# Latent-attention heads turned in groups of 128 columns in a two-layer encoder trunk

## The chip, the cores and the metric

The kernel runs on one core of a Trainium2 chip. The metric is the device time of one execution in microseconds (us), the median of several runs. A profiled execution gives the trace from which the rows are quoted. Its span is the time from the first to the last recorded instruction; the time of the execution is a little longer than its span.

The engines are called as the profile calls them: PE (TensorE, matrix products), PEld (its weight loads, which overlap the products), ACT (ScalarE), DVE (VectorE), POOL (GpSimd), SP (SyncE, which issues the loads). PE writes to PSUM, which has eight banks of 128 partitions x 512 floats; ACT and DVE copy results from there to SBUF, POOL works in SBUF alone.

## The reference

One sequence of 512 tokens with 1024 features goes through two layers. All of it is float32.

```python
h = rms_norm(x, attn_norm_g[l])
proj = h @ w_in[l]
c_q, c_kv, k_rope, gq, gk, gv, pool_in, gate_logits = split_columns(proj, IN_SIZES)
o_mla  = mla_branch(...)     # latent attention, 8 heads
o_gqa  = gqa_branch(...)     # 8 query heads of 64, 2 key heads
o_pool = pool_branch(...)    # centred means over 2/4/8/16 tokens, minus the token
gates = sigmoid(gate_logits).reshape(b, s, 3, d)
merged = sum of gates[:, :, i] * (branch i @ its projection)
x = x + merged @ w_out[l]
hf = rms_norm(x, ffn_norm_g[l])
u = depthwise_conv(hf @ ffn_w_up[l], ffn_conv_w[l], ffn_conv_b[l])
x = x + (silu(u_gate) * u_val) @ ffn_w_down[l]
```

In the latent attention each head of q and of k has 96 features, 64 without position and 32 rotary ones:

```python
q = (rms_norm(c_q, q_norm_g) @ w_uq).reshape(b, s, 8, 96)
kv = (rms_norm(c_kv, kv_norm_g) @ w_ukv).reshape(b, s, 8, 64 + 64)
k_nope, v = kv[..., :64], kv[..., 64:]
k = concatenate([k_nope, k_rope for every head], axis=-1)
q = rms_norm(q, qh_g); k = rms_norm(k, kh_g)
q, k: the last 32 features rotated by the token's row and column
o = softmax(q k^T * 96 ** -0.5) v
```

## The kernel before

Every product is made from halves: an operand is rounded to a shorter format (the high half, by a copy on ACT or DVE, line 208 or 231), and the rest is subtracted (the low half, on DVE or POOL, line 215 or 219). `mm3` then issues three matmuls: high x high, high x low, low x high. Weights are loaded as `raw` by SP, split into `wh` and `wl` by `w_split` some pieces ahead, and used once. Activations lie as feature x token in XM, HH (high) and HL (low), in eight chunks of 128 features.

A layer goes through these stages. First the latents: eight chunks of weights times HH and HL into four banks, token x feature. Then four groups of the pool branch; in layer 0 the sum of squares for the first norm (`norm_finish`, a product of `ones` with `sq`) is put between the matmuls of the first group, because the norm's factor is applied to results only afterwards. `rt` is that factor per token, `rbc` the same spread over partitions. Then the latents are normed (`mx`) and turned, and the grouped-query columns follow. Then comes grouped-query attention, beside which PE works on the gates and projection of the pool branch; then latent attention, beside which it works on those of the grouped-query branch; then the last gates, the output projection, the convolution network.

For latent attention `make_q` and `make_n` write the heads, token x feature, to MQ and MK, two tiles of four heads each, in time with the gates before. `q_norm` and `k_norm` scale them and apply the rotation on POOL. `t_q(h)` and `t_k(h)` later turn one head into features x tokens: four transposes of 128 tokens each into the one bank `mi`, then a high half (`qa`, `kh`) and a low half (`qb`, `kl`). `gcol` is a factor per feature put on q when it is copied. `m_row` uses the same bank for the row of the scores' maxima. `t_pair` does the same for two heads of the grouped-query branch, whose 128 columns are turned at once.

The order of the instructions is written out by the program itself: a model of the engines' times (`Clock`) keeps a heap of due steps; `chain` runs a list of steps one after the other, `need` waits until a result is due, `ps(tag)` until a bank of that tag is free. The list `plan` in `attention` gives a position for each step of each head. Between steps, units of the gates and branches (`Filler`) are issued up to a target, and up to SLACK = 35 units beyond it while the next step's inputs are not yet due. `copy` puts a copy on ACT or on DVE, whichever the model has free earlier, and `pick` does so with a low half between DVE and POOL. Banks: two each of `acc`, `ST` and `AV`, one each of `S` and `mi`. Each engine runs its own instructions strictly in the order in which the program issued them.

Of the kernel before, what the change touches and what calls it, by code (L numbers as in the profile page):

```python
# [18 lines left out]
P = 128  # L19
# [37 lines left out]
def _order(br):  # L57
# [189 lines left out]
def trunk(ctx: ExitStack, tc: tile.TileContext, x, w, prm, gb, cst, out):  # L247
# [41 lines left out]
    def f(ap):  # L289
        return ap.bitcast(F32)  # L290
# [14 lines left out]
    def w_split():  # L305
        j = st["split"]
        sl, off, wd = pieces[j]
        r = raws[sl][:, off:off + wd]
        hi = hlp.tile([P, T], F32R, tag="wh", name=f"wh{j}")
        lo = hlp.tile([P, T], F32R, tag="wl", name=f"wl{j}")  # L310
        ck.fin = ck.now
        A.activation(hi[:, :wd], r, AF.Copy)
        e = V if j < KC + 3 else pick(W_BIAS, ck.fin + ck.SEM)
        ck.free[e.kind] = max(ck.free.get(e.kind, 0.0), ck.fin + ck.SEM)
        e.tensor_tensor(lo[:, :wd], r, f(hi[:, :wd]), ALU.subtract)
        done("w", j)
        halves[j] = (hi, lo)
        st["split"] += 1
# [191 lines left out]
    def layer(l, sq, xsrc):  # L510
# [9 lines left out]
        tabs = [slot("tabg"), slot("tabg")]  # L520
        tabm = slot("tabm")

        gcol = small("gcol", [P, 1], bufs=1)

        def tables():
            V.tensor_tensor(gcol[0:96], pr[0:96, PRM_MQ:PRM_MQ + 1], pr[0:96, PRM_MQ + 1:PRM_MQ + 2], ALU.mult)
            V.tensor_scalar(gcol[0:64], gcol[0:64], 96.0 ** -0.5, None, ALU.mult)
            V.tensor_scalar(gt[:, 0:128], gt[:, 0:128], 64.0 ** -0.5, None, ALU.mult)
# [398 lines left out]

        def q_norm(g):
            q = MQ[g]
            qr = q[:, :, :, 64:96]  # L930
            cs, sn = (tabm[:, o:o + 128].rearrange("p (b f) -> p b f", b=4)[:, :, None, :] for o in (0, 128))
            r2 = slot("rp2")[:, :T].rearrange("p (b h f) -> p b h f", b=4, h=4)
# [5 lines left out]
            def part(o, i):  # L938
                G.tensor_tensor(r2[:, :, :, o:o + 16], qr[:, :, :, i:i + 16], bc(sn[:, :, :, o:o + 16], [P, 4, 4, 16]),
                                ALU.mult)  # L940

            return [lambda: scale(0), lambda: scale(1), lambda: part(0, 16), lambda: part(16, 0),
                    lambda: G.tensor_tensor(qr, qr, bc(cs, [P, 4, 4, 32]), ALU.mult),
                    lambda: G.tensor_tensor(qr, qr, r2, ALU.add), lambda: done("mq", l, g)]

        def make_n(g):
            wh, wl = wnext()
# [24 lines left out]
        def n_out(g, p, acc):  # L972
            j = slot("mns")
            bs = slice(2 * p, 2 * p + 2)

            def copies():
                copy(MK[g][:, bs, :, 0:64], acc.rearrange("p (b h f) -> p b h f", b=2, h=4))
                A.activation(j[:, :T], acc, AF.Square)
                free("acc")

            def sums():
                V.tensor_reduce(ss[:, 1, g, bs], j[:, :T].rearrange("p (b h f) -> p b h f", b=2, h=4), AX.X, ALU.add)
                done("ssn", l, g, p)

            chain(copies, sums)

        def k_norm(g):
            k = MK[g]

            def nope(p):  # L990
                bs = slice(2 * p, 2 * p + 2)
                G.tensor_tensor(k[:, bs, :, 0:64], k[:, bs, :, 0:64], bc(ss[:, 1, g, bs].unsqueeze(3), [P, 2, 4, 64]),
                                ALU.mult)

            def rope():
                G.tensor_tensor(k[:, :, :, 64:96], bc(krr[:, :, None, :], [P, 4, 4, 32]),
                                bc(ss[:, 1, g].unsqueeze(3), [P, 4, 4, 32]), ALU.mult)

            return [([("krr", l)], rope), lambda: nope(0), lambda: nope(1), lambda: done("mk", l, g)]

# [36 lines left out]
        def attention(kind, fill, okey, odst):  # L1037
# [7 lines left out]
            def t_q(h):  # L1045
                if gqa:
                    return t_pair(h) if h % 2 == 0 else None
                s = hs[h] = {}
                tp = ps("mi")
                need(("mq", l, h // 4))  # L1050
                for b in range(4):
                    turn(tp[0:96, b * P:b * P + P], MQ[h // 4][:, b, h % 4, :])
                qa, qb = s["qa"], s["qb"] = slot("qa", F32R), slot("qb", F32R)

                def hi():
                    A.activation(qa[0:96, :T], tp[0:96], AF.Copy, scale=gcol[0:96])

                def lo():
                    V.scalar_tensor_tensor(qb[0:96, :T], tp[0:96], gcol[0:96], f(qa[0:96, :T]), ALU.mult, ALU.subtract)
                    free("mi")  # L1060
                    done(*key("q", h))

                chain(hi, lo)

            def t_pair(h):

# [6 lines left out]
                for i in range(2):  # L1073
# [18 lines left out]
            def t_k(h):  # L1092
                if gqa:
                    return
                s = hs[h]
                need(("mk", l, h // 4))
                tp = ps("mi")
                for b in range(4):
                    turn(tp[0:96, b * P:b * P + P], MK[h // 4][:, b, h % 4, :])
                ka, kb = s["ka"], s["kb"] = slot("kh", F32R), slot("kl", F32R)  # L1100

                def hi():
                    copy(ka[0:96, :T], tp[0:96])
                    G.memset(f(ka[96:100, :T]), 1.0)
                    done(*key("kh", h))

                def lo():
                    V.tensor_tensor(kb[0:96, :T], tp[0:96], f(ka[0:96, :T]), ALU.subtract)
                    free("mi")
                    done(*key("kl", h))  # L1110

                chain(hi, lo)

            def s_max(h, b):
                s = hs[h]
# [365 lines left out]
def _pack_weights(i):  # L1481
    res = []
    for l in range(L):
# [16 lines left out]
        for br in (2, 1, 0):  # L1500
            for k, m in _order(br):
# [3 lines left out]
                elif k == "b":  # L1505
                    res += _cut(_blocks(wb[br][:, c], 4))
                elif k == "q":
                    res += [uq[kc * P:kc * P + P, m * 384:m * 384 + 384] for kc in range(2)]
# [19 lines left out]
def _pack_params(i):  # L1528
# [3 lines left out]
    def ones_after(v):  # L1532
# [3 lines left out]
    prm = np.concatenate([cols(i["attn_norm_g"]), cols(i["ffn_norm_g"]), cols(i["pool_scale"]),  # L1536
                          cols(i["mla_q_norm_g"]), cols(i["mla_kv_norm_g"]),
                          cols(cw[:, 0]), cols(cw[:, 1]), cols(cw[:, 2]), cols(i["ffn_conv_b"]),
                          cols(ones_after(i["mla_q_head_g"])), cols(ones_after(i["mla_k_head_g"]))], axis=2)

    def swap(v):
        n = v.shape[1] // 2
# [56 lines left out]
```

## Time and profile before

| | |
|---|---|
| median of 3 runs | 1649.69 us (1648.71 to 1650.75) |
| the profiled execution, its time | 1649.25 us |
| its span | 1647.3 us |
| granted TensorE clock | 1.00 |
| instructions | 20363 |
| PE matmuls | 7435 |
| POOL busy | 921.9 us (56%) |
| DMA queue of the weights | 143.97 MB, 27.6% of 16 engines |

The stages lie about here (us of the span): latents, pool and grouped-query columns 0 to 98, grouped-query attention to 212, latent attention 226 to 354, the rest of layer 0 up to 819; layer 1 repeats it. In a timeline row the columns are start, duration, engine, line, operation, output<-inputs, shape, count, and in brackets how long the engine was idle before and for whom. A matmul's duration overlaps that of the next; what a matmul costs is the distance between two starts. In a row of waits stand who waited and for whom, us in total, times, and the longest.

### The profile page before, as it was taken

What the parts mean: (1) busy time and instruction counts of PE and PEld (TensorE: products, weight loads), DVE (VectorE), ACT (ScalarE), POOL (GpSimd) and SP (SyncE); (2) the same over time, 40 slices, a digit from 0 to 9 for tenths busy, and PEclk for the clock granted to TensorE, in tenths of its full rate; (3) what the DMA queues carried; (4) which work ended last, traced back from release to release, by engine and by line L of the source; (5) the groups of instructions that cost most, each with busy time, mean ns of one, the idle gap of its engine ahead of it and who ended that gap; (6) DMA issues with size and microseconds to landing.
All of it is one profiled execution on the core that took longest, in us unless ns stands there. A gap on an engine that the chain in (4) does not pass through costs nothing.

```text
span 1647.3 us, 20363 instructions
## 1 busy us (share of the span) xinstructions
PE 1640.4 (100%) x7435; PEld 1336.7 (81%) x7435; DVE 890.5 (54%) x1404; ACT 761.8 (46%) x1357; POOL 921.9 (56%) x805
## 2 busy tenths in 40 slices
PE   9999999999999999999999999999999999999999
PEld 8887887778888888888888888877788888888888
DVE  6777756643366666621046677566332666666000
ACT  6457745543444444432244577455434444444221
POOL 3762763344666666654568538534446656656542
PEclk9999999999999999999999999999999999999999
DMA  5221121123322323333332211211243232332331
GB/s 201 82 84 46 60 65 48 52 71 118 119 90 90 103 90 91 102 102 122 102 103 89 82 39 62 74 39 52 85 133 95 85 103 90 91 101 90 126 111 45
DMA packets 44739, 145.40 MB, mean 88 GB/s; under 512 B 5088, under 2 KB 6624, under 8 KB 44640
## 3 DMA queue, kind: packets, MB, share of 16 engines
q1 hardware_dynamic: 44352, 143.97, 27.6%
q8 instruction: 59, 0.97, 0.2%
q14 instruction: 40, 0.33, 0.1%
q10 hardware_dynamic: 288, 0.14, 0.0%
HBM read 139.90 MB, written 4.19 MB: 87 GB/s over the span
## 4 chain that ended last, share of the span: by engine, by line
PE 98%; DVE 1%; ACT 1%; DMA 0%; SPq 0%; issue 0%
PE ps_acc L344 44%; PE ps_AV L344 24%; PE ps_ST L344 23%; PE ps_S L344 4%; PE ps_mi L344 2%; PE ps_mi L348 1%; DVE sq L215 0%; DMA XM<-x 0%; ACT wh L208 0%; ACT sqt L208 0%; DVE wl L215 0%; PE ps_acc L348 0%; SPq L301 0%; ACT HH L208 0%; SPq L1439 0%
## 5 line engine op out<-in xcount | busy, mean ns | idle before, releaser
L215 POOL TENSOR_TENSOR wl<-raw,wh 128x512 fp32r<-128x512 f32 (+2 forms) x508 | 662.9, 1315 | 589.0 <-ACT wh L208 457.7
L208 ACT ACTIVATE wh<-raw 128x512 fp32r<-128x512 f32 (+3 forms) x522 | 308.8, 607 | 125.6 <-PE ps_ST L344 41.1
L219 DVE SCALAR_TENSOR_TENSOR a<-u,prm,a 128x512 f32<-128x512 f32 x176 | 238.9, 1358 | 79.4 <-ACT a L208 73.2
L344 PE MATMUL ps_acc<-HH,wh 128*128 128x512 f32 x592 | 234.7, 396 | 1.4 <-DVE XM L219 1.4
L344 PE MATMUL ps_acc<-HL,wh 128*128 128x512 f32 x592 | 234.6, 396 | 0.0
L344 PE MATMUL ps_acc<-HH,wl 128*128 128x512 f32 x592 | 234.2, 396 | 0.0
L344 PEld LDWEIGHTS ps_acc<-HH,wh 128*128 128x128 f32 x592 | 111.5, 188 | 28.5 <-ACT mqs L208 1.7
L344 PEld LDWEIGHTS ps_acc<-HH,wl 128*128 128x128 f32 x592 | 111.3, 188 | 26.3
L344 PEld LDWEIGHTS ps_acc<-HL,wh 128*128 128x128 f32 x592 | 111.5, 188 | 25.5
L208 ACT ACTIVATE ps_ST<-ps_ST 128x512 f32<-128x512 f32 x128 | 74.6, 583 | 113.5 <-PE ps_ST L344 113.0
L344 PE MATMUL ps_AV<-HL,wh 128*128 128x512 f32 x288 | 114.2, 396 | 0.0
L344 PE MATMUL ps_AV<-HH,wl 128*128 128x512 f32 x288 | 114.2, 396 | 0.0
L344 PE MATMUL ps_AV<-HH,wh 128*128 128x512 f32 x288 | 113.6, 394 | 0.0
L223 DVE TENSOR_REDUCE nm<-ps_S 128x1 fp32r<-128x512 f32 x128 | 87.8, 686 | 42.4 <-PE ps_S L344 41.1
L215 DVE TENSOR_TENSOR pl<-ps_ST,ph 128x512 fp32r<-128x512 f32 x128 | 87.7, 685 | 38.4 <-ACT ph L208 37.4
L215 POOL TENSOR_TENSOR al<-a,ah 128x512 fp32r<-128x512 f32 x44 | 58.2, 1322 | 84.9 <-ACT ah L208 58.6
L344 PE MATMUL ps_ST<-HL,wh 128*128 128x512 f32 x240 | 95.3, 397 | 0.0
L344 PE MATMUL ps_ST<-HH,wl 128*128 128x512 f32 x240 | 95.0, 396 | 0.0
L344 PE MATMUL ps_ST<-HH,wh 128*128 128x512 f32 x240 | 94.6, 394 | 0.0
L208 ACT ACTIVATE a<-u,prm 128x512 f32<-128x512 f32 x88 | 71.8, 815 | 33.4 <-DVE u L215 33.4
L208 ACT ACTIVATE ah<-a 128x512 fp32r<-128x512 f32 x44 | 27.8, 631 | 116.0 <-DVE u L243 110.6
L208 ACT ACTIVATE a<-a 128x512 f32<-128x512 f32 x44 | 27.8, 632 | 113.0 <-DVE u L243 113.0
(361 smaller groups left out, 3543.8 us busy)
## 6 DMA issues: line engine op xcount, KB each, us to landing
raw<-w SPq DMA_DIRECT2D x228, 512.0 KB, 3.5
raw<-w SPq DMA_DIRECT2D x13, 384.0 KB, 3.1
XM<-x SPq DMA_DIRECT2D x16, 256.0 KB, 4.1
raw<-w SPq DMA_DIRECT2D x6, 448.0 KB, 3.4
xsp<-XM SPq DMA_DIRECT2D x8, 256.0 KB, 2.0
XM<-xsp SPq DMA_DIRECT2D x8, 256.0 KB, 3.4
out<-XM SPq DMA_DIRECT2D x7, 256.0 KB, 2.1
raw<-w SPq DMA_DIRECT2D x4, 432.0 KB, 3.1
```

The lines of the kernel that those rows point to most:

```text
L208: return self.eng.activation(out, in_, func, **k)
L215: return self.eng.tensor_tensor(out, *a)
L219: return self.eng.scalar_tensor_tensor(out, *a)
L223: return self.eng.tensor_reduce(out, in_, *a, **k)
L344: PE.matmul(o, lhsT=lhsT, rhs=rhs, start=start, stop=stop)
L348: PE.transpose(o, src, ident)
```

## The change

Six things are changed.

1. `t_q` and `t_k` turn the columns of four heads in three groups of 128 and not in four of 96. The head h with h % 4 == 3 has no transposes of its own. A group holds one whole head and a third of the next (group 0), two thirds of two heads (group 1), or a third of one and a whole head (group 2). TURNS lists for each group which head gets which rows, and at which row of the head they go. In every second head the 32 rotary columns stand ahead of the other 64, so that all pieces begin at a multiple of 32 and end up in the same rows of the head as before. The weights of q are permuted for that outside the kernel; for k, `parity` picks the columns.
2. All high halves of a group are made first, then all low ones, in one chain; then the bank is freed. The pieces of 32 rows of q have no factor, the others take it from `gcol`, which gets a second column in the groups' order.
3. `q_norm` and `k_norm` do on POOL in two steps, for even and odd heads, what was one step: for q both parts of the rotation, the product with the cosines and the sum, for k the scaling. The copies of k into MK are split in the same way.
4. The two copies per pair of grouped-query heads (`t_pair`) are always on ACT, not on ACT or DVE.
5. In layer 0 the norm's sum comes after six chunks of the first pool group, not four.
6. The high half of the very first piece of weights is made on DVE, not ACT, and the twelve products of the first chunk are issued as four high x high, four low x high, four high x low, and not bank by bank.

```diff
-NPRM = PRM_MQ + 2
+NPRM = PRM_MQ + 4
+TURNS = (((0, 0, 96, 0), (1, 96, 128, 64)), ((1, 0, 64, 0), (2, 64, 128, 0)),
+         ((2, 0, 32, 64), (3, 32, 64, 64), (3, 64, 128, 0)))
 # w_split
-        A.activation(hi[:, :wd], r, AF.Copy)
+        if j == 0:
+            V.tensor_copy(hi[:, :wd], r)
+        else:
+            A.activation(hi[:, :wd], r, AF.Copy)
 # tok_major
+                if st["use"] == 1:
+                    for n, (x_, w_) in enumerate(((HH, wh), (HL, wh), (HH, wl))):
+                        for b in range(4):
+                            mm(banks[b][:, :wd], x_[:, kc, b * P:b * P + P], w_[:, :wd], n == 0, False)
+                    continue
 # layer, the pool groups
-                if l == 0 and g == 0 and n == 3:
+                if l == 0 and g == 0 and n == 5:
                     norm_finish(G1, sq, nrm)
 # q_norm
+            def part(o, j):
...
+                for i in range(2):
+                    G.tensor_tensor(hold[0][:, i, :, :, o:o + 16], pair(i)[:, :, :, j:j + 16],
+                                    bc(sn[:, :, :, o:o + 16], [P, 4, 2, 16]), ALU.mult)
+            def turned():
+                for i in range(2):
+                    G.tensor_tensor(pair(i), pair(i), bc(cs, [P, 4, 2, 32]), ALU.mult)
+            def add():
+                for i in range(2):
+                    G.tensor_tensor(pair(i), pair(i), hold[0][:, i], ALU.add)
 # n_out
-                copy(MK[g][:, bs, :, 0:64], acc.rearrange("p (b h f) -> p b h f", b=2, h=4))
+                for e in range(2):
+                    copy(parity(MK[g][:, bs], e, 32 * e, 64),
+                         acc.rearrange("p (b i e f) -> p b i e f", b=2, i=2, e=2)[:, :, :, e])
 # k_norm, nope
+                for e in range(2):
+                    v = parity(k[:, bs], e, 32 * e, 64)
+                    G.tensor_tensor(v, v, bc(inv(e)[:, bs].unsqueeze(3), [P, 2, 2, 64]), ALU.mult)
 # t_q
+                j, h0 = h % 4, h - h % 4
+                if j == 3:
+                    return
+                need(("mq", l, h // 4))
+                tp = group(MQ[h // 4], j)
+                for n, a, z, o in TURNS[j]:
...
+                    src, w = tp[a:z], z - a
+                    qa, qb = s["qa"][o:o + w, :T], s["qb"][o:o + w, :T]
+                    g = None if w == 32 else gcol[0:96, 0:1] if w == 96 else gcol[a:z, 1:2]
...
+                chain(*his, *los, lambda: free("mi"))
+            def group(heads4, j):
                 tp = ps("mi")
                 for b in range(4):
-                    turn(tp[0:96, b * P:b * P + P], MQ[h // 4][:, b, h % 4, :])
+                    turn(tp[:, b * P:b * P + P], heads4[:, b].rearrange("p h f -> p (h f)")[:, j * P:j * P + P])
+                return tp
 # t_pair
-                        copy(qa[own, :T], tp[own])
+                        A.activation(qa[own, :T], tp[own], AF.Copy)
 # t_k
+                for n, a, z, o in TURNS[j]:
+                    s = hs[h0 + n]
+                    if "ka" not in s:
+                        s["ka"], s["kb"] = slot("kh", F32R), slot("kl", F32R)
+                        his.append(lambda ka=s["ka"]: G.memset(f(ka[96:100, :T]), 1.0))
...
+                chain(*his, *los, lambda: free("mi"))
 # the weights of q, packed outside
+                    c = np.concatenate([np.roll(np.arange(96), 32 * (h % 2)) + 96 * h for h in range(4 * m, 4 * m + 4)])
```

More of the change, by code (lines that the diff above doesn't have):

```diff
@@ L929, in q_norm @@
             q = MQ[g]
-            qr = q[:, :, :, 64:96]
             cs, sn = (tabm[:, o:o + 128].rearrange("p (b f) -> p b f", b=4)[:, :, None, :] for o in (0, 128))
-            r2 = slot("rp2")[:, :T].rearrange("p (b h f) -> p b h f", b=4, h=4)
+            hold = []
             def scale(p):
@@ L936, in scale, with pair, parity @@
                 G.tensor_tensor(q[:, bs], q[:, bs], bc(ss[:, 0, g, bs].unsqueeze(3), [P, 2, 4, 96]), ALU.mult)
-            def part(o, i):
-                G.tensor_tensor(r2[:, :, :, o:o + 16], qr[:, :, :, i:i + 16], bc(sn[:, :, :, o:o + 16], [P, 4, 4, 16]),
-                                ALU.mult)
+            def pair(i):
+                return q.rearrange("p b h f -> p b (h f)")[:, :, 192 * i + 64:192 * i + 128].rearrange(
+                    "p b (e f) -> p b e f", e=2)
+            def part(o, j):
+                if not hold:
+                    hold.append(slot("rp2")[:, :T].rearrange("p (i b e f) -> p i b e f", i=2, b=4, e=2))
+                for i in range(2):
[7 more added lines that the diff above has]
+                    G.tensor_tensor(pair(i), pair(i), hold[0][:, i], ALU.add)
             return [lambda: scale(0), lambda: scale(1), lambda: part(0, 16), lambda: part(16, 0),
-                    lambda: G.tensor_tensor(qr, qr, bc(cs, [P, 4, 4, 32]), ALU.mult),
-                    lambda: G.tensor_tensor(qr, qr, r2, ALU.add), lambda: done("mq", l, g)]
+                    turned, add, lambda: done("mq", l, g)]
+        def parity(k, e, o, n):
+            return k.rearrange("p b h f -> p b (h f)").rearrange("p b (i x) -> p b i x", i=2)[
+                :, :, :, 96 * e + o:96 * e + o + n]
         def make_n(g):
@@ L988, in k_norm, with inv @@
             k = MK[g]
+            def inv(e):
+                return ss[:, 1, g].rearrange("p b (i e) -> p b i e", e=2)[:, :, :, e]
             def nope(p):
                 bs = slice(2 * p, 2 * p + 2)
-                G.tensor_tensor(k[:, bs, :, 0:64], k[:, bs, :, 0:64], bc(ss[:, 1, g, bs].unsqueeze(3), [P, 2, 4, 64]),
-                                ALU.mult)
+                for e in range(2):
+                    v = parity(k[:, bs], e, 32 * e, 64)
+                    G.tensor_tensor(v, v, bc(inv(e)[:, bs].unsqueeze(3), [P, 2, 2, 64]), ALU.mult)
             def rope():
-                G.tensor_tensor(k[:, :, :, 64:96], bc(krr[:, :, None, :], [P, 4, 4, 32]),
-                                bc(ss[:, 1, g].unsqueeze(3), [P, 4, 4, 32]), ALU.mult)
+                for e in range(2):
+                    G.tensor_tensor(parity(k, e, 64 * (1 - e), 32), bc(krr[:, :, None, :], [P, 4, 2, 32]),
+                                    bc(inv(e).unsqueeze(3), [P, 4, 2, 32]), ALU.mult)
             return [([("krr", l)], rope), lambda: nope(0), lambda: nope(1), lambda: done("mk", l, g)]
@@ L1047, in t_q, with hi, lo @@
                     return t_pair(h) if h % 2 == 0 else None
-                s = hs[h] = {}
+                j, h0 = h % 4, h - h % 4
[3 more added lines that the diff above has]
+                tp = group(MQ[h // 4], j)
+                his, los = [], []
+                for n, a, z, o in TURNS[j]:
+                    s = hs.setdefault(h0 + n, {})
+                    if "qa" not in s:
+                        s["qa"], s["qb"] = slot("qa", F32R), slot("qb", F32R)
+                    src, w = tp[a:z], z - a
+                    qa, qb = s["qa"][o:o + w, :T], s["qb"][o:o + w, :T]
+                    g = None if w == 32 else gcol[0:96, 0:1] if w == 96 else gcol[a:z, 1:2]
+                    def hi(src=src, qa=qa, g=g):
+                        A.activation(qa, src, AF.Copy, **({} if g is None else {"scale": g}))
+                    def lo(src=src, qa=qa, qb=qb, g=g, h=h0 + n, whole=j == 2 or w == 96 or o == 0 and n == 1):
+                        if g is None:
+                            V.tensor_tensor(qb, src, f(qa), ALU.subtract)
+                        else:
+                            V.scalar_tensor_tensor(qb, src, g, f(qa), ALU.mult, ALU.subtract)
+                        if whole:
+                            done(*key("q", h))
+                    his.append(hi)
+                    los.append(lo)
+                chain(*his, *los, lambda: free("mi"))
+            def group(heads4, j):
                 tp = ps("mi")
-                need(("mq", l, h // 4))
                 for b in range(4):
-                    turn(tp[0:96, b * P:b * P + P], MQ[h // 4][:, b, h % 4, :])
[L1053 to L1063, printed above, removed]
+                    turn(tp[:, b * P:b * P + P], heads4[:, b].rearrange("p h f -> p (h f)")[:, j * P:j * P + P])
+                return tp
             def t_pair(h):
@@ L1094, in t_k, with hi, lo @@
                     return
-                s = hs[h]
+                j, h0 = h % 4, h - h % 4
+                if j == 3:
+                    return
                 need(("mk", l, h // 4))
[L1097 to L1112, printed above, removed]
+                tp = group(MK[h // 4], j)
+                his, los = [], []
+                for n, a, z, o in TURNS[j]:
[3 more added lines that the diff above has]
+                        his.append(lambda ka=s["ka"]: G.memset(f(ka[96:100, :T]), 1.0))
+                    src, w = tp[a:z], z - a
+                    ka, kb = s["ka"][o:o + w, :T], s["kb"][o:o + w, :T]
+                    whole = j == 2 or w == 96 or o == 0 and n == 1
+                    def hi(src=src, ka=ka, h=h0 + n, whole=whole):
+                        copy(ka, src)
+                        if whole:
+                            done(*key("kh", h))
+                    def lo(src=src, ka=ka, kb=kb, h=h0 + n, whole=whole):
+                        V.tensor_tensor(kb, src, f(ka), ALU.subtract)
+                        if whole:
+                            done(*key("kl", h))
+                    his.append(hi)
+                    los.append(lo)
+                chain(*his, *los, lambda: free("mi"))
             def s_max(h, b):
@@ L1507, in _pack_weights @@
                 elif k == "q":
-                    res += [uq[kc * P:kc * P + P, m * 384:m * 384 + 384] for kc in range(2)]
+                    c = np.concatenate([np.roll(np.arange(96), 32 * (h % 2)) + 96 * h for h in range(4 * m, 4 * m + 4)])
+                    res += [uq[kc * P:kc * P + P, c] for kc in range(2)]
                 else:
@@ L1538, in _pack_params @@
                           cols(cw[:, 0]), cols(cw[:, 1]), cols(cw[:, 2]), cols(i["ffn_conv_b"]),
-                          cols(ones_after(i["mla_q_head_g"])), cols(ones_after(i["mla_k_head_g"]))], axis=2)
+                          *[cols(z) for g in (i["mla_q_head_g"], i["mla_k_head_g"])
+                            for z in (ones_after(g), np.concatenate([g[:, :64]] * 2, axis=1))]], axis=2)
     def swap(v):
```

5 lines of the change are left out of this document (3 added, 2 removed).

## The prediction

> **What bounds the kernel now.** I read the page's engine shares and its chain of waits first, then who PE waited for.
>
> ```profile
> PE 1640.4 (100%) x7435; PEld 1336.7 (81%) x7435; DVE 890.5 (54%) x1404; ACT 761.8 (46%) x1357; POOL 921.9 (56%) x805
> PE 98%; DVE 1%; ACT 1%; DMA 0%; SPq 0%; issue 0%
> PE ps_acc L344 <- DVE XM L219: 1.4, 1, 1.4
> PE ps_mi L1436 <- DVE ones L243: 1.1, 1, 1.1
> PE ps_S L344 <- DVE sq L215: 0.6, 1, 0.6
> PE ps_acc L344 <- DVE vml L215: 0.4, 2, 0.2
> PE ps_acc L344 <- DVE wl L215: 0.2, 1, 0.2
> ```
>
> PE is on 98% of the chain, and all its waits but that for the ones of the warm-up come to 2.6 us. So there are two ways to get faster: give PE fewer instructions, or take away one of these waits. Work added to the other engines costs time only where it makes a new PE wait. The change has a part of each kind.
>
> **Fewer transposes.** By instruction source, line L348 holds the transposes; after it stand pieces of PE's timeline (start, duration, instruction): one group of MQ, and one of the grouped-query heads, which already turns 128 columns.
>
> ```profile
> L348 PE MATMUL ps_mi<-C,MQ x64: 270/272/274, 226.5 to 1132.4; 128*96 128x128 f32 x64
> L348 PE MATMUL ps_mi<-C,MK x64: 271/273/275, 229.0 to 1142.8; 128*96 128x128 f32 x64
> 226.50 0.60 PE L348 MATMUL ps_mi<-C,MQ 128*96 128x128 f32 x4
> 226.86 0.48 PE L344 MATMUL ps_acc<-HH,wh 128*128 128x512 f32 x1
> 227.18 0.40 PE L344 MATMUL ps_acc<-HL,wh 128*128 128x512 f32 x1
> 227.41 0.40 PE L344 MATMUL ps_acc<-HH,wl 128*128 128x512 f32 x1
> 102.85 0.60 PE L348 MATMUL ps_mi<-C,gqr 128*128 128x128 f32 x4
> 103.21 0.48 PE L344 MATMUL ps_acc<-HH,wh 128*128 128x512 f32 x1
> 103.52 0.40 PE L344 MATMUL ps_acc<-HL,wh 128*128 128x512 f32 x1
> ```
>
> There are 128 transposes of latent features: 32 groups of four, one group for each of 8 heads, for q and k, in 2 layers. A group takes 226.86 - 226.50 = 0.36 us until the next matmul starts, and that one's successor comes 0.32 us later where 0.23 (227.41 - 227.18) is normal: 0.36 + 0.09 = 0.45 us of PE. The group of 128 columns takes 0.36 + (0.31 - 0.23) = 0.44. So a transpose costs the same for 96 and for 128 columns. Three groups instead of four for each four heads make 24 groups of 32, and 8 x 0.44 = **3.5 us** leave PE. Nothing hides them, as PE is the chain.
>
> **The norm sum two chunks later.** PE and DVE around it, and the row that later comes closest:
>
> ```profile
> 25.17 0.40 PE L344 MATMUL ps_AV<-HH,wl 128*128 128x512 f32 x1
> 26.18 1.05 PE L344 MATMUL ps_S<-ones,sq 128*128 128x2 f32 x8 [0.61 <-DVE sq L215]
> 40.53 3.99 DVE L227 TENSOR_SCALAR mx<-mx,ssc 128x256 f32<-128x256 f32 x8 [0.92 <-POOL ssc L215]
> 47.23 1.03 PE L348 MATMUL ps_acc<-C,mx 128*128 128x128 f32 x8
> ```
>
> At the normal pitch the sum would start at 25.17 + 0.23 = 25.40; it starts at 26.18, when DVE's last square is added. Two chunks are six matmuls, 1.4 us: PE would reach the sum at 26.80, after the squares. The wait of **0.78 us** is gone. What hangs on the sum comes 26.80 - 26.18 = 0.62 us later and is wanted 0.78 earlier, together 1.40. The latents end at 40.53 + 3.99 = 44.52 and are turned at 47.23, a slack of 2.7: 1.3 is left, no new wait.
>
> **The first weights.** DVE and PE at the start:
>
> ```profile
> 4.52 0.75 DVE L219 SCALAR_TENSOR_TENSOR HL<-XM,prm,HH 128x512 fp32r<-128x512 f32 x1 [3.47 <-ACT HH L208]
> 5.11 0.52 PE L344 MATMUL ps_acc<-wh,HH 128*128 128x384 f32 x1
> 7.50 0.55 DVE L215 TENSOR_TENSOR wl<-raw,wh 128x384 fp32r<-128x384 f32 x1
> 7.82 0.34 PE L344 MATMUL ps_acc<-wh,HH 128*128 128x384 f32 x1
> 8.10 0.44 PE L344 MATMUL ps_acc<-wl,HH 128*128 128x384 f32 x1
> L231 DVE CAST ka<-ka x4: 411/639/876, 99.1 to 918.9; 64x512 fp32r<-64x512 f32 x4
> ```
>
> The rounding of the first weights goes to DVE, where it is queued behind HL (the program's due times put HL at 4.01 and the weights at 4.05, and the trace has that order), so it starts at 5.27. SBUF to SBUF it takes 0.41 to 0.88 (the ka row): wh is there at 5.7 to 6.15, and PE's first matmul comes 0.6 to 1.0 later than 5.11. Then chunk 0 runs without a hole, since its twelve matmuls in the new order want HL and wl only after four and eight of them. Twelve take about 2.1 us (0.23 x 384/512 = 0.17 each), so chunk 1 begins at 7.8 to 8.25 instead of 7.82. But chunk 1 waits for its own wl at 8.10, made by DVE from 7.50 to 8.05 behind the arrival of x, which the edit doesn't touch. So it gains nothing and costs 0 to 0.3; I take **0**, as DVE has nothing else to do there. The two more parameter columns ride in a load needed much later: 0.
>
> **Query copies on ACT.** DVE and PE in the grouped-query stage of layer 0:
>
> ```profile
> 148.04 0.69 DVE L231 CAST qa<-ps_mi 64x512 fp32r<-64x512 f32 x1 [0.71 <-ACT qa L208]
> 150.94 0.69 DVE L219 SCALAR_TENSOR_TENSOR XM<-gt,ps_acc 128x512 f32<-128x512 f32 x1
> 151.78 0.47 PE L344 MATMUL ps_acc<-HH,wh 128*128 128x512 f32 x1 [1.44 <-DVE XM L219]
> ```
>
> PE's longest wait is for an acc bank which the XM product on DVE frees at 151.63. Ahead of that product in DVE's queue stands this cast: DVE stood 0.71 us until ACT had copied the other head from the same bank, then copied for 0.69. On ACT the copy goes behind ACT's own, and DVE has 1.40 us less before the product; but ACT's next outputs, on which DVE's following steps wait, come about 0.6 later. So the gain lies between 0 and the whole 1.44. I take **0.7**, the cast alone. Of three such casts in the trace the other two stand before no PE wait: 0. (The Trainium skill, page PSUM — Partial Sum Buffer, section Terms, speaks of a collision for two engines in one bank and quadrant; these two heads lie in different quadrants, and here DVE waited all the same.)
>
> **More pieces around each group.** Costs of one evacuation, by tile (ns minimum/median/maximum), and the load of the engines in 32 us of latent attention and in 40 us of the grouped-query stage (from:to, us, then PE, PEld, DVE, ACT, POOL busy):
>
> ```profile
> L208 ACT ACTIVATE qa<-ps_mi,gcol x16: 673/683/686, 227.1 to 1132.7; 96x512 fp32r<-96x512 f32 x16
> L219 DVE SCALAR_TENSOR_TENSOR qb<-ps_mi,gcol,qa x16: 664/736/747, 227.9 to 1134.0; 96x512 fp32r<-96x512 f32 x16
> L215 DVE TENSOR_TENSOR kl<-ps_mi,kh x16: 674/676/687, 230.4 to 1143.9; 96x512 fp32r<-96x512 f32 x16
> 258.00:290.00 32.00, 32.00 (x148) 25.44 (x147) 20.94 (x34) 18.67 (x35) 13.78 (x12) 1.00 0.11 34
> 140.00:180.00 40.00, 38.56 (x184) 31.39 (x183) 30.45 (x49) 29.25 (x55) 20.58 (x28) 1.00 0.15 47
> 184.54 1.30 POOL L215 TENSOR_TENSOR MQ<-MQ,rp 128x512 f32<-128x512 f32 x1
> 211.06 2.04 POOL L215 TENSOR_TENSOR MK<-MK,ssm 128x512 f32<-128x512 f32 x2
> L215 POOL TENSOR_TENSOR rp<-MQ,tabm x8: 732/742/768, 178.0 to 1011.1; 128x256 f32<-128x256 f32 x8
> L215 POOL TENSOR_TENSOR MQ<-MQ,tabm x4: 1282/1296/1301, 182.0 to 1011.9; 128x512 f32<-128x512 f32 x4
> ```
>
> The three groups of four heads are read in 2 + 2 + 3 = 7 pieces where four heads had 4. Per layer that is 6 more high parts for q and 6 for k (0.68 at most each, about 8 us, mostly ACT) and 12 more low parts on DVE (6 x 0.74 + 6 x 0.68 = 8.5 us). Spread over the some 100 us in which heads are turned, DVE goes from 20.94 of 32 (65%) to about 74%, ACT from 58% to 66%. That is no new bound; it is the load of 140 to 180, where DVE has 30.45 of 40 (76%) and PE its one wait. A group also holds the single mi bank for two or three pieces on either engine instead of one, about 4.2 us (3 x 0.68 + 3 x 0.74) for the longest; queued behind that are the row of maxima (which shares the bank) and the next group. The issue order answers by drawing gate and branch matmuls forward, and it does so until 35 units past its target, about 24 us at 0.7 each. So latency becomes earlier filler and not a PE hole. What can reach PE is a burst on DVE that delays the release of an acc bank. Bounds: 0 (258 to 290 has PE at 32.00 of 32) and, at the rate of the grouped-query stages (1.44 us of waits in two stages of about 114 us), 1.3 us in 200; I take **+0.6**.
>
> POOL: the halves of the rotary steps cost 2 x 0.74 where a whole was 1.30, the two parts of each similar, so about 0.6 us for four heads of q and, for k's split steps, less; some 2 us a layer. Cover: MQ of the first four heads is done at 185.84 and first turned at 226.50; MK at 213.10 and first turned at 229.0. The 40 and 16 us hide it. The split copies of k into MK cost about 0.2 us for each of four outputs on ACT or DVE, hidden in the same way.
>
> **The sum.** The profiled execution took 1649.25 us (span 1647.3), 0.44 under the median of the runs, 1649.69. 1649.25 - 3.5 - 0.78 - 0.7 + 0.6 = 1644.9 on its own scale, **1645.3 us** against the median.
>
> **Rivals.** *Bursts eat part of the gain.* DVE's two or three low parts in a row come ahead of a product or a logit as the cast did at 148; four or five such waits of 0.7 instead of one make +3 us: 1647.7 us. For it speaks that DVE gets the load of 140 to 180; against it that in that load PE waited once.
>
> *Columns, not groups, cost.* 16 x 4 x 96 and 12 x 4 x 128 are both 6144 columns a layer; were a transpose paced by them, the 3.5 us would stay: 1648.8 us. Against it: 0.36 us at 226.50 with 96 and at 102.85 with 128. (The Trainium skill, page TensorE: Matmul & The Clock Gate, section "LDWEIGHTS (loading the stationary operand)", has a weight load grow with its columns alone; by that rule as the pace this rival would hold, and the trace disagrees.)
>
> *Slower.* The three-piece group is the place. If the two further low parts of each stand before an acc release with no slack left, 4 such groups x 2 parts x 2 layers = 16 ops x 0.7 = 11 us come onto PE: 1645.3 - 0.6 + 11 = 1655.9. It decides from 12 ops (8.4 us, more than 4.4 + 3.3 + the 0.6 allowed). For it speaks the single mi bank and the serial order of pieces; against it that the two acc banks give each product the 2.8 us of a branch (12 matmuls x 0.23) before PE wants its bank, which a burst of 2.1 fits into.
>
> *Not done as said*: the deferred sum or the copy leaves PE's waits (0.78 and 1.44) where they are: 1646.8.
>
> **How the numbers follow.** Forecast 0.67, bursts 0.15, columns 0.04, slower 0.08, not done 0.06. About 0.2%, 3.3 us, is what a measurement of this kernel can tell from no change: the line lies at 1646.4. The forecast's own range is 1643.0 (the whole 1.44 saved, no new wait, runs 0.6 low) to 1646.4; with bursts to 1648.5. **Range 1642.8 to 1648.5**. Faster by over 0.2%: 0.68; within: 0.24; slower: 0.08.
>
> **What would show it.** Right: 48 transposes each on MQ and MK at a 0.36 us group; the sum on PE with no wait; no DVE cast of qa from mi; no PE wait over 0.5 us between 226 and 354 or in the same stage of layer 1; PE's time in each latent attention shorter by four groups, 1.8 us. Wrong: PE waits for acc or mi with DVE qb, kl or XM named, a wait at the latents' transposes, or a PE hole before chunk 1's wl that is longer than 0.3.

## The result and the profile after

The changed kernel takes 1653.93 us (median of 10 runs, 1653.21 to 1654.26), against 1649.16 for the kernel before on the same chip (10 runs, 1648.65 to 1650.75): ratio 1.0027 [1.0018, 1.0037]. It is slower, and the forecast of 1645.3 us with its range to 1648.5 was wrong. The profiled execution took 1653.78 us (span 1651.8, clock 1.00), 4.53 more than the one of before.

The page after, engine shares and chain by engine:

```profile
PE 1641.0 (99%) x7403; PEld 1330.8 (81%) x7403; DVE 914.4 (55%) x1433; ACT 780.4 (47%) x1386; POOL 927.4 (56%) x833
PE 97%; ACT 1%; DVE 1%; issue 0%; DMA 0%; DVEq 0%
```

PE has the 32 instructions less that were forecast (7403 for 7435), yet the span is 4.5 us longer. Who PE waited for in the kernel after (total us, times, longest):

```profile
PE ps_AV L352 <- ACT ph L213: 2.0, 4, 0.6
PE ps_S L352 <- DVE nm L228: 1.6, 2, 0.8
PE ps_mi L352 <- DVE nm L228: 1.6, 2, 0.8
PE ps_mi L1503 <- DVE ones L248: 1.1, 1, 1.1
PE ps_acc L352 <- DVE vml L220: 0.5, 2, 0.3
PE ps_acc L352 <- DVE XM L224: 0.5, 1, 0.5
PE ps_acc L352 <- DVE wh L236: 0.4, 1, 0.4
```

The first three rows are new: 5.2 us in eight waits, four in each layer. None is for a bank held by a late DVE part, as the forecast had feared. They are for `nm` (the row maxima) and `ph` (the high halves of the exponentials), steps of the attention itself. All four of layer 0 lie in one stretch of PE's timeline (start, duration, instruction, idle before):

```profile
342.52 0.39 PE L352 MATMUL ps_acc<-HH,wl 128*128 128x512 f32 x1
...
343.69 0.40 PE L352 MATMUL ps_ST<-qa,kh 100*128 100x512 f32 x1
344.89 0.50 PE L352 MATMUL ps_S<-kh,qa 96*128 96x512 f32 x1 [0.80 <-DVE nm L228]
345.23 0.40 PE L352 MATMUL ps_AV<-ph,vmh 128*128 128x512 f32 x1
...
347.81 0.22 PE L352 MATMUL ps_mi<-idr,nm 128*4 128x128 f32 x1 [0.78 <-DVE nm L228]
...
353.11 0.50 PE L352 MATMUL ps_AV<-ph,vmh 128*128 128x512 f32 x1 [0.41 <-ACT ph L213]
...
356.35 0.50 PE L352 MATMUL ps_AV<-ph,vmh 128*128 128x512 f32 x1 [0.61 <-ACT ph L213]
...
357.41 0.40 PE L352 MATMUL ps_acc<-HH,wh 128*128 128x512 f32 x1
```

Between the first and the last row there is no gate or branch matmul, the "filler" that PE does while the other engines work on a head. These 14.9 us are the last head of the layer, and its steps stand bare. Of its 45 steps from one start to the next, 44 at the usual 0.233 and one of 0.06 (the matmul of `nm`) would take 10.3 us, so the waits, and the slower starts around them (0.34 and 0.39 in place of 0.23), cost **4.6 us**. Before, filler stood between the steps to the end of the stage:

```profile
352.80 0.40 PE L344 MATMUL ps_acc<-HH,wl 128*128 128x512 f32 x1
...
353.50 0.39 PE L344 MATMUL ps_AV<-pl,vmh 128*128 128x512 f32 x1
353.73 0.39 PE L344 MATMUL ps_acc<-HH,wh 128*128 128x512 f32 x1
```

The busy time of that window, 340 to 358, in the kernel before (PE, PEld, DVE, ACT, POOL):

```profile
340.00:358.00 18.00, 18.00 (x79) 14.29 (x78) 6.91 (x11) 9.79 (x17) 5.67 (x5) 1.00 0.20 59
```

And after, with the window in which the forecast had read the engines' load:

```profile
340.00:358.00 18.00, 15.40 (x60) 9.80 (x59) 10.73 (x17) 12.86 (x24) 3.71 (x3) 1.00 0.07 28
258.00:290.00 32.00, 32.00 (x144) 25.22 (x144) 23.51 (x38) 18.84 (x33) 13.52 (x12) 1.00 0.15 47
```

While the heads are turned (258 to 290) PE still has no gap, with DVE at 23.51 of 32 (73%; 74% was forecast) and ACT at 18.84 (59%; 66% was forecast). The loss is only at the end.

By stage, with marks that both kernels have: from the first group of MQ to the second norm's sum (`ps_S<-ones,sq`, one per layer) layer 0 took 461.52 - 226.50 = 235.0 us before and 463.00 - 225.01 = 238.0 after, layer 1 235.3 and 238.2. That is 3.0 a layer: 4.6 us of holes less some 1.7 for the missing transposes. Two layers make +5.9. By the first group of MQ the kernel after is 1.5 us ahead (225.01 for 226.50), through the small edits (parts 4 to 6 of the change; the kernel that has these alone, below, stands at 224.89). 5.9 - 1.5 = 4.4, of the 4.53 measured.

### The profile page after: what moved, and what is told of

Read it like the earlier page. It is cut to its first block, busy times and chain, and to the rows that moved or that the text cites. A ratio compares the mean times of both kernels' runs of the same rounds, so it can differ in the third digit from the quotient of the medians.

```text
span 1651.8 us, 20386 instructions
## 1 busy us (share of the span) xinstructions
PE 1641.0 (99%) x7403; PEld 1330.8 (81%) x7403; DVE 914.4 (55%) x1433; ACT 780.4 (47%) x1386; POOL 927.4 (56%) x833
## 4 chain that ended last, share of the span: by engine, by line
PE 97%; ACT 1%; DVE 1%; issue 0%; DMA 0%; DVEq 0%
PE ps_acc L352 44%; PE ps_AV L352 24%; PE ps_ST L352 23%; PE ps_S L352 4%; PE ps_mi L352 2%; PE ps_mi L356 1%; ACT ps_ST L213 0%; ACT ph L213 0%; DVE nm L228 0%; DMA prm<-prm 0%; DVE pl L220 0%; ACT osum L213 0%; ACT oraw L213 0%; PE ps_acc L356 0%; DVE vmh L236 0%
## 5 line engine op out<-in xcount | busy, mean ns | idle before, releaser
L213 ACT ACTIVATE wh<-raw 128x512 fp32r<-128x512 f32 (+1 forms) x521 | 309.0, 608 | 126.3 <-PE ps_ST L352 41.4
```

The costliest lines, as they stand in the source:

```text
L213: return self.eng.activation(out, in_, func, **k)
```

## The theory and its rivals

**A, the stock.** Filler is finite. The program has 116 units a layer; 17 are used before the stage, and the other 99 at some 0.7 us each, about 69 us of PE's work, have to last for 127 us of attention. A group now holds the single `mi` bank for up to six pieces in a row, and for k also for a POOL memset put into the same chain. The issue order bridges the wait for `mi` by drawing filler, up to 35 units too early. Besides, `t_q` and `t_k` of the fourth heads (3 and 7) issue nothing any more, but `waits` still names `mi` for `t_q`, so these empty steps draw filler too. Counted in the instruction order that the program writes, the steps of q drew 5 units a layer before and 41 after, 16 of these at the two empty steps; and the stock ends after the first of the four pieces of head 7's maxima. The trace shows such a draw at the first heads. Kernel before, first group of k and second of q:

```profile
229.04 0.60 PE L348 MATMUL ps_mi<-C,MK 128*96 128x128 f32 x4
231.80 0.60 PE L348 MATMUL ps_mi<-C,MQ 128*96 128x128 f32 x4
```

Kernel after:

```profile
229.63 0.60 PE L356 MATMUL ps_mi<-C,MK 128*128 128x128 f32 x4
237.98 0.60 PE L356 MATMUL ps_mi<-C,MQ 128*128 128x128 f32 x4
238.34 0.48 PE L352 MATMUL ps_S<-kh,qa 96*128 96x512 f32 x1
```

2.8 us lie between the two groups before and 8.4 after, nearly all filled with gate and branch matmuls, so no wait is seen.

**B, a small edit.** One of the three small edits costs the time. Then the kernel with these alone would be slow, and the one with the grouped transposes alone fast.

**C, the pieces.** The longer evacuations themselves (more parts on ACT and DVE, `mi` held longer) make `nm` and `ph` late. Then they would be late in any issue order with these pieces, and on time without them. (The expectations below use these letters.)

## The experiments

Medians in us; ratios are to the kernel before on the same chip (its medians there were 1649.02 to 1649.16). "Bare" is the longest stretch without filler in layer 0's latent attention, "layer" the time between the two marks above in layer 0.

| kernel | median | ratio | bare | layer |
|---|---|---|---|---|
| before | 1649.16 | 1 | 3.0 | 235.0 |
| after | 1653.93 | 1.0027 [1.0018, 1.0037] | 14.9 | 238.0 |
| small edits alone | 1648.19 | 0.9994 [0.9985, 1.0002] | 3.0 | 235.0 |
| grouped transposes alone | 1656.31 | 1.0043 [1.0031, 1.0056] | 15.1 | 238.6 |
| after, empty steps don't wait | 1648.01 | 0.9993 [0.9984, 1.0002] | 4.2 | 235.2 |
| and memset apart, q turned later ("new order") | 1645.47 | 0.9978 [0.9969, 0.9986] | 3.5 | 233.7 |
| before, filler drawn early | 1658.2 | 1.0057 [1.0044, 1.0070] | 12.7 | 239.0 |
| after, SLACK 6 | 1666.54 | 1.0109 [1.0094, 1.0125] | 3.5 | 241.2 |
| after, memset apart | 1649.54 | 1.0001 [0.9992, 1.0010] | 4.7 | 235.6 |
| after, 24 filler pieces | 1655.49 | 1.0043 [1.0030, 1.0055] | 6.3 | 238.1 |
| grouped transposes, new order | 1645.98 | 0.9982 [0.9973, 0.9991] | 3.5 | 233.7 |
| after, SLACK 6 in latent attention | 1661.47 | 1.0074 [1.0061, 1.0087] | 3.5 | 240.8 |
| new order, old first weights | 1645.43 | 0.9978 [0.9969, 0.9987] | 3.5 | 233.7 |
| empty steps and memset, q as it was | 1649.53 | 1.0003 [0.9994, 1.0012] | 4.7 | 235.9 |

**Which part loses: the small edits alone.** The kernel before with parts 4, 5 and 6 of the change (cut; the new order of the first chunk's products is in it too):

```diff
+        if j == 0:
+            V.tensor_copy(hi[:, :wd], r)
...
-                if l == 0 and g == 0 and n == 3:
+                if l == 0 and g == 0 and n == 5:
...
-                        copy(qa[own, :T], tp[own])
+                        A.activation(qa[own, :T], tp[own], AF.Copy)
```

> The kernel before with the three small edits alone (query copies on ACT, norm sum two chunks later, first weights on DVE with the first chunk's new order); heads are turned as before. Theory A (filler drawn early: the grouped transposes hold the bank mi longer, the issue order waits for it by issuing gate and branch matmuls, and the last head of each layer is left without any): this kernel keeps before's gain, 1649.2 - 0.7 (norm) - 1.0 (copy) = 1647.5 us, no PE wait in the latent attention. Theory B (one of the small edits costs the time): over 1650.

1648.19, 0.9 us under the kernel before on its chip (1649.09), not separable from none by its interval; no holes. Theory B is out.

**The grouped transposes alone.** The kernel after with those three edits undone, that is the same lines with + and - exchanged.

> The grouped transposes alone, the three small edits undone. Theory A: 8 groups less (-3.5) and the holes at the last head (+4.8 in each layer): 1649.2 + 6.1 = 1655.3 us, with PE waits for nm and ph at the end of both latent attentions. Theory B: 1646.

1656.31, with a bare stretch of 15.1: the whole loss is here. The two parts do not add up exactly: +7.2 and -0.9 make 6.3, where the whole change has 4.8. The layer is 0.6 longer here than in the kernel after (238.6 and 238.0); 0.3 of that is a longer wait for `nm` (1.1 and 0.8), the rest is left open.

**The empty steps.** The kernel after, with one line in `waits`:

```diff
+                if not gqa and fn in (t_q, t_k) and h % 4 == 3:
+                    return [], None
```

> The changed kernel, but the issue order no longer waits for the bank before the steps of the fourth and eighth head, which issue nothing (9 and 7 units of gates and branches were drawn there in each layer by the program's own count). Theory A: 16 units (11 us of PE) are left for the last head and the holes shrink from 4.8 to about 1.5 in each layer: 1653.9 - 6.6 = 1647.3 us. Theory C (the longer chains of pieces and DVE's load make the last head late by themselves, whatever filler there is): same as changed, 1653.9.

1648.01: 5.9 us come back, more than the 4.8 that the change had lost, through an edit that touches no instruction of the transposes and none of their pieces. Against C. One wait a layer is left in this kernel:

```profile
PE ps_AV L352 <- ACT ph L213: 1.2, 2, 0.6
```

**The order made right.** That edit, the memset of k in a chain of its own, and the position for turning q in the plan at -1.9 in place of -2.351, that is later:

```diff
-                        his.append(lambda ka=s["ka"]: G.memset(f(ka[96:100, :T]), 1.0))
+                        chain(lambda ka=s["ka"]: G.memset(f(ka[96:100, :T]), 1.0))
...
-        "mla": (-2.351, 0.028, 1.098, 0.64, 3.303, 1.678, 1.82, 33.91)}
+        "mla": (-1.9, 0.028, 1.098, 0.64, 3.303, 1.678, 1.82, 33.91)}
```

> As the one that skips the idle steps, and with the memset of k's rows of ones taken out of the chain that holds the bank, and q's group placed 0.45 of a step later in the plan, so that nothing is drawn at q's groups any more. Theory A: filler lasts to the end, no hole; 1649.2 - 3.5 - 0.7 - 1.0 = 1644.0 us. Theory C: the holes stay for the most part, 1650 or more.

1645.47, faster than both kernels, with all pieces of the change. That this is the time forecast for the change is partly luck: the forecast took 4.4 us off a median of 1649.69, and here 3.6 come off 1649.09 (this run's own expectation was 1644.0). Its waits of PE hold neither `nm` nor `ph`:

```profile
PE ps_mi L1505 <- DVE ones L248: 1.1, 1, 1.1
PE ps_acc L352 <- DVE vml L220: 0.5, 2, 0.3
PE ps_acc L352 <- DVE XM L224: 0.5, 1, 0.5
PE ps_acc L352 <- DVE wh L236: 0.4, 1, 0.4
```

**The loss without the change.** The decisive one: the kernel before, no piece of the change in it, with five units of filler issued ahead of each turned head but the first.

```diff
+                if not gqa and fn is t_q and args[0] > 0:
+                    for _ in range(5):
+                        fill.step()
```

> The kernel before, nothing of the change; only five units of gates and branches more are issued ahead of each turned head of the latent attention but the first (35 a layer, about what the changed kernel draws at q's groups). All the work is the same. Theory A (filler used up early makes the holes, whatever used it): PE waits for nm and ph at the last head of both layers, 4 to 6 us each: 1649.1 + 10 = 1659 us. Theory C (the pieces make the holes): 1649 to 1650.

1658.2: early filler alone makes the holes, of the same kinds. Its waits, and the filler-free stretch (346.38 to 359.03) with one of them:

```profile
PE ps_AV L344 <- ACT ph L208: 2.0, 4, 0.6
PE ps_mi L344 <- DVE nm L223: 1.6, 2, 0.8
```

```profile
346.38 0.39 PE L344 MATMUL ps_acc<-HH,wl 128*128 128x512 f32 x1
...
349.43 0.22 PE L344 MATMUL ps_mi<-idr,nm 128*4 128x128 f32 x1 [0.78 <-DVE nm L223]
...
359.03 0.40 PE L344 MATMUL ps_acc<-HH,wh 128*128 128x512 f32 x1
```

Even the lengths agree with those after (2.0 and 1.6 in total, 0.78 in the row); only the wait of `ps_S` for `nm` is missing. Layer 0 takes 239.0 us for 235.0. C is out: early filler without the pieces makes the holes, and the pieces in an order that keeps filler to the end make none.

**Three other cures, two of them misses.** SLACK 6 for 35 in the kernel after:

```diff
-SLACK = 35
+SLACK = 6
```

> The changed kernel with SLACK 6 for 35: the issue order may run at most six units ahead of its target and otherwise issues the step although its bank or input is not due. Theory A: filler lasts to the end, no holes at the last head, but PE now stands where q's groups wait for the bank, six of them a layer at 2 to 4 us less what six units cover: 1649 to 1655. Theory C: holes at the last head as in the changed kernel.

1666.54, a miss. The bare stretch is gone (3.5), but the limit acts in the grouped-query stage too (the first group of MQ comes at 227.57, not 225.01), and in latent attention PE now waits at the groups. With the limit only there:

```diff
-                while fill.done < target + SLACK and waiting(fn, *args) and fill.step():
+                while fill.done < target + (SLACK if gqa else 6) and waiting(fn, *args) and fill.step():
```

> The changed kernel with the limit of six units ahead in the latent attention alone; the grouped-query stage keeps its 35. Of the 12.6 us that the limit everywhere cost against the changed kernel, some 2.5 in each layer were in the grouped-query stages by the start of the latent attention (227.57 for 225.01): 1666.5 - 5 = 1661.5 us, with no hole at the last head and PE waits for mi and nm at the groups. Theory C: holes at the last head as well.

1661.47, as expected, and the waits stand at the groups and maxima:

```profile
PE ps_mi L352 <- DVE nm L228: 4.2, 4, 1.2
PE ps_mi L356 <- DVE kl L220: 3.0, 6, 0.8
PE ps_S L352 <- DVE nm L228: 2.8, 4, 0.8
```

So drawing filler early is right for the next step and wrong for the last one: saving it costs more here than spending it. The wait for the bank has to be made shorter, not left unbridged. The third cure gives the stage more filler, 24 pieces of a gate in place of 16 (`2 * KC`), the third gate of the last branch moved ahead:

```diff
-            for _ in range(2 * KC):
+            for _ in range(24):
...
-        fb = Filler(beside(), units(1) + 2 * KC)
+        fb = Filler(beside(), units(1) + 24)
```

> The changed kernel with eight units more of filler (a third gate of the last branch moved ahead, 5.6 us of PE work, no work added). Theory A: the holes shrink by some of these 5.6 us in each layer: 1649 us. Theory C: 1653.9.

1655.49, a miss. The bare stretch falls from 14.9 to 6.3, but the third gate had been the cover of what comes after the attention. PE waits there now, for the output of the last head:

```profile
364.35 0.51 PE L352 MATMUL ps_acc<-oh,wh 128*128 128x512 f32 x1 [1.85 <-ACT oh L213]
```

**The memset alone, and a new wait.** The kernel after with only the memset in a chain of its own (the first two lines of the diff above with the memset):

> The changed kernel with one edit: the memset of k's rows of ones is no step of the chain that holds the bank any more (issued on its own). Theory A: the chain is 1 to 2 us shorter in the program's reckoning, some 9 units fewer are drawn at q's groups by its count and the filler lasts to the last head's last block: holes of about 1 us a layer, 1646.5 us. Theory C: 1653.9.

1649.54, a miss by 3. At the last head no stretch is over 3.5 any more; the longest, 4.7, now lies at 241, at a wait that each layer has and that no kernel above had at this length:

```profile
PE ps_acc L352 <- DVE vml L220: 3.8, 4, 1.7
```

Both edits of the order, without the later turning of q:

> Idle steps skipped and the memset out of the chain, the plan's positions as in the change. 17 units are still drawn at q's groups by the program's count, and filler lasts to the end: no hole at the last head, 1645.5 us, unless another early filler unit meets its bank too soon as with the memset alone (1.7 us a layer, then 1648).

1649.53, the second of its two outcomes: the same wait, though the empty steps no longer draw. The later turning is worth 4.1 us (1645.47), since with it PE has no wait at this place. PE, DVE and POOL of this kernel there:

```profile
241.18 0.40 PE L352 MATMUL ps_acc<-HH,wl 128*128 128x512 f32 x1
243.23 0.36 PE L352 MATMUL ps_acc<-wh,cth 128*128 128x256 f32 x1 [1.65 <-DVE vml L220]
```

```profile
240.21 1.40 DVE L220 TENSOR_TENSOR wl<-raw,wh 128x512 fp32r<-128x512 f32 x1
241.63 0.68 DVE L220 TENSOR_TENSOR qa<-ps_mi,C 4x512 fp32r<-4x512 f32 x1
242.33 0.76 DVE L220 TENSOR_TENSOR vml<-ps_acc,vmh 128x256 fp32r<-128x256 f32 x2
```

```profile
239.76 1.29 POOL L220 TENSOR_TENSOR XM<-XM,gt 128x512 f32<-128x512 f32 x1
```

DVE frees the acc bank with `vml`, and in front of it stand a low half of weights, which the order had put on DVE, and a row of the head. The kernels with the later turning have 14 low halves of weights on DVE; this one and the one with the memset alone have 16, and the two more stand at these two waits, one in each layer (here at 240.21 and 1058.73). This is the burst on DVE that the forecast had feared for an acc bank; it came with this order, not with the change as it was made.

**What each part is worth.** The new order without the three small edits, and with the first weights as they were:

> The grouped transposes with the repaired order (idle steps skipped, memset out of the chain, q's group 0.45 later), but without the three small edits: what the transposes alone are worth. By the prediction's price 8 x 0.44 = 3.5 us: 1649.1 - 3.5 = 1645.6. By the difference that the repaired kernel had to the small edits alone, 2.7: 1646.4. Theory C (the pieces themselves cost as much as the transposes save): 1649.

> The repaired kernel with the edit of the first weights undone as well: chunk 1's second product at 8.10 for 8.38, 0.2 us: 1645.3 us, the same within a measurement.

1645.98: the grouped transposes by themselves, once no filler is lost, save 3.0 us (interval of the ratio 0.9973 to 0.9991), where 3.5 was forecast. 1645.43: the first weights on DVE are worth nothing that can be told.

## Why the prediction was wrong

**The step that failed** is "So latency becomes earlier filler and not a PE hole". The first half held. The second took filler for unlimited: a unit drawn early is missing at the end of the layer, where the last head then stands bare. The forecast had the bank's hold at 4.2 us a group and SLACK at 24 us, and didn't add the draws up against the 99 units. Its allowance for new waits of +0.6 had to be 9.2 (two times 4.6). By the timed runs it is 8.5: the kernel after (1653.93) against the same pieces in the new order (1645.47). It also had no term for the steps of the fourth heads, which issue nothing, though `waits` names a bank for them; taking that wait away brought 5.9 us back.

**The rivals.** *Slower* was right in sign and near in size (1655.9), but by luck, as its place was another: between 226 and 340 the trace names no PE wait at all, for an acc bank or anything else. *Bursts* had the same place, and foretold a gain. *Not done as said* did not occur: the sum's wait is gone, and no cast of `qa` from `mi` on DVE is left. *Columns* is refuted by the 3.0 us that the grouped transposes save in the new order, by the 0.36 us from a group of 128 columns to the next start (237.98 to 238.34 above), and by the new rows of the transposes, 48 each and of the old duration:

```profile
L356 PE MATMUL ps_mi<-C,MQ x48: 270/272/273, 225.0 to 1134.4; 128*128 128x128 f32 x48
L356 PE MATMUL ps_mi<-C,MK x48: 270/272/275, 229.6 to 1144.9; 128*128 128x128 f32 x48
```

Two sums of the prediction are off, and nothing hangs on them: the lower end of its own range comes to 1643.4 by its terms (1645.3 - 0.74 - 0.6 - 0.6), not 1643.0, and *Slower* needs 11.2 for its 16 x 0.7 to make 1655.9.

**Right.** *Transposes:* 235.0 to 233.7 us in the layer in the new order, 1.3 where 1.8 was said; 3.0 in the timed runs where 3.5 was said. *The norm sum:* no wait is left of the 0.78, and the distance from the matmul before the sum's place is one pitch:

```profile
26.74 0.40 PE L352 MATMUL ps_AV<-HH,wl 128*128 128x512 f32 x1
26.97 0.95 PE L352 MATMUL ps_S<-ones,sq 128*128 128x2 f32 x8
27.78 0.48 PE L352 MATMUL ps_AV<-HH,wh 128*128 128x512 f32 x1
```

With six matmuls (1.40) after the sum moved ahead of it, the kernel before would have been at 27.09 + 1.40 = 28.49 in place of 27.78 (27.09: the first matmul after its sum). That is 0.71 from trace to trace, and traces of the same code differ here by more, as the first weights show. *The query copies:* the wait at XM went from 1.44 to 0.47, which is 0.97 where 0.7 was said:

```profile
150.15 0.47 PE L352 MATMUL ps_acc<-HH,wh 128*128 128x512 f32 x1 [0.47 <-DVE XM L224]
```

*The first weights:* 0 was said, 0 to 0.3 allowed. PE's first product comes 0.59 later (5.70 for 5.11), as said. Chunk 1's second product starts at 8.38 where it started at 8.10, but the end of the chunk before the norm's sum differs by up to 0.9 us between traces of the same code (24.89 in the kernel before with filler drawn early, 25.77 in the grouped transposes in the new order), so the trace can't price it; the timed runs say 0. *POOL:* MQ and MK of the first four heads are written at 185.4 and 212.0 and first turned at 225.01 and 229.63; no wait shows there. The small edits alone save 0.9 in the timed runs, where the trace of the kernel after has 1.5 by the first group of MQ; the difference lies within what traces of one code vary by and is left open.

## What to carry to other kernels

Work that an issue order draws forward to bridge a wait is a stock: add up what a change draws, against the stock, and look at the end of the stage, not at the place of the change, for the hole. When a step becomes empty, take its waits out of the order as well. And when filler runs out, shorten the hold that draws it: neither holding it back (1661 us) nor borrowing from the next stage (1655) brought the time below that of the kernel before.

## What the runs showed of the hardware

The DVE subtraction `wl` of two SBUF operands (128x512) in the rows above took 1.40 us, while POOL worked on two SBUF operands (239.76 to 241.05) for the larger part of it. Early in the same trace, when POOL had not yet begun its work (its first low halves start at 20.55), the same subtraction took 0.68:

```profile
18.31 0.68 DVE L220 TENSOR_TENSOR wl<-raw,wh 128x512 fp32r<-128x512 f32 x1
```

So `wl` is 0.7 us longer beside POOL, and that is a part of what makes `vml` late. The overlap was seen, not tried by itself.

A matmul after a wait costs 0.2 to 0.3 us beyond the wait that the trace names. It starts 1.20 after the one before it (343.69 to 344.89) with 0.80 named as waiting, where 0.23 is usual: 0.17 more. And the next start comes 0.34 later (344.89 to 345.23), again 0.11 more. The four waits in the bare stretch have 2.6 us named and lost 3.7 in this way; the rest of the 4.6 are short gaps between starts (0.31 to 0.39), for which the trace names no wait.

The transposes' cost of 0.36 us a group, from its start to the next matmul's, did not move from 96 to 128 columns, though each weight load did, from 125 ns to 140 by the loads' rows, before:

```profile
L348 PEld LDWEIGHTS ps_mi<-C,MQ x64: 122/125/129, 226.3 to 1132.3; 128*96 128x96 f32 x64
```

and after:

```profile
L356 PEld LDWEIGHTS ps_mi<-C,MQ x48: 138/140/146, 224.8 to 1134.3; 128*128 128x128 f32 x48
```
